# Two blocks on one core: 128 of the 192 tiles of `w_ada` are issued by GpSimd's DMA queue instead of SyncE's

## The chip, the cores and the metric

The kernel runs on one core of one Trainium2 chip. The metric is the device time of one execution in microseconds (us), lower is better. All data is float32 (the engines also use float32r, a form of it that the matrix engine takes in one pass).

## What is computed

The program runs two blocks, one after the other, on 256 tokens of width 2048. The first block is conditioned by a vector `c`: one product `silu(c) @ w_ada + b_ada` gives six rows of 2048 numbers, which shift, scale and gate the two halves of the block. Cut to what matters here:

```
cond = jax.nn.silu(c)
mod = cond @ w_ada[i] + b_ada[i]                      # w_ada: 2048 x 12288
shift1, scale1, gate1, shift2, scale2, gate2 = jnp.split(mod, 6, axis=-1)
h = _modulate(_rms(x, norm1_w[i]), shift1, scale1)
u, q, k, v = jnp.split(h @ w_in[i], splits, axis=-1)
y_ssm = _s5_mixer(u, ...)                             # a scan over the tokens
y_att = _dilated_attention(q, k, v, ...)
x = x + gate1 * (jnp.concatenate([y_ssm, y_att], -1) @ w_out[i])
h2 = _modulate(_rms(x, norm2_w[i]), shift2, scale2)
x = x + gate2 * ((jax.nn.silu(h2 @ w_ffn_gate[i]) * (h2 @ w_ffn_up[i])) @ w_ffn_down[i])
```

The second block has a conditioning product of its own (`ada_w_2`), an attention over the tokens and a context, and a Fourier mixer. All of it works on weights that are read from HBM once.

## The kernel before

**The work on weights.** A weight tile is 512 KB: 256 rows by 512 columns, as 128 partitions by 2 by 512. `gemm` (line 237) walks over the rows; for each tile `wtile` (line 210) loads it into a buffer of the tag `raw` (line 214, issued by SyncE, `SY`), and `split` (line 176) makes two float32r tiles of it: ScalarE casts it into `wh` (line 177), VectorE takes the rest, `wl = raw - wh` (line 178). TensorE then makes twelve products of 128x512 with each tile (line 133). There are three buffers of `wh` and three of `wl`, so at most three split tiles exist at a time. In parts of the first block, weights are used whole, without the split: `full_tile` (line 204) loads them into `wh` or `wl` (line 207).

**The work on the conditioning.** A tile of `w_ada` is also 512 KB and also lives in a `raw` buffer: five buffers (`T["raw"]`) serve both kinds. Tiles are consumed in three ways:

- `ada_tiles` (line 798, issue at line 806) makes the first shift and scale, 64 tiles at the start of the program;
- `ada_gen` (line 296, issue at line 306) takes 128 rows by 1024 columns; VectorE multiplies the tile by one column of `silu(c)` and adds it into an accumulator `acc` (line 278; the first one at line 276). 96 tiles of `w_ada` go this way: both gates, and half of the second shift and scale;
- `ada_quad` (line 347, issue at line 353) takes 256 rows by 512 columns and lets TensorE multiply them, four rows of tokens at a time; 32 tiles of `w_ada`, the other halves of the second shift and scale.

The same `ada_gen` then reads 192 tiles of `ada_w_2` for the second block.

**What sets the order.** `ada_all` (line 383) is a generator, a "lane", that yields after each tile; the loops over weights call `tick()` (line 195) after each weight tile, which advances the lane at a rate set for each stage. In the stage of the hidden layer (`w_ffn_gate`, `w_ffn_up`) the rate is 0.5: one tile of `w_ada` for two weight tiles. The order of the instructions on each engine, and which of the five `raw` buffers a tile gets, are then decided by a scheduler that sorts the program by its own estimates. At run time each engine and each DMA queue takes its instructions strictly in that order, and a DMA into a `raw` buffer waits for the last reader of what lay in it before.

Of the kernel before, what the change touches and what calls it, by code (L numbers as in the profile page):

```python
# [81 lines left out]
def kernel(ctx: ExitStack, tc: tile.TileContext, A, out):  # L82
    nc = tc.nc
    V, S, G, PE, SY = nc.vector, nc.scalar, nc.gpsimd, nc.tensor, nc.sync
# [14 lines left out]
    def uname(s):  # L99
        count[0] += 1  # L100
        return f"{s}_{count[0]}"
# [30 lines left out]
    def mm(o, l, r, start, stop):  # L132
        PE.matmul(o, l, r, start=start, stop=stop)  # L133
# [23 lines left out]
    def rsqrt(src, scale, shape, key="r"):  # L157

        w, y, t, yi = (small(shape, key + n, d) for n, d in (("w", F32), ("y", F32), ("t", F32), ("i", I32)))
        V.tensor_scalar(out=w, in0=src, scalar1=float(scale), scalar2=EPS, op0=ALU.mult, op1=ALU.add)  # L160
        V.tensor_scalar(out=yi, in0=w.bitcast(I32), scalar1=1, scalar2=None, op0=ALU.logical_shift_right)
        V.tensor_scalar(out=yi, in0=yi, scalar1=-1, scalar2=0x5F3759DF, op0=ALU.mult, op1=ALU.add)
        V.tensor_scalar(out=w, in0=w, scalar1=-0.5, scalar2=None, op0=ALU.mult)
        y0 = yi.bitcast(F32)
        for i in range(3):
            if shape[1] == 1:
                V.tensor_scalar(out=t, in0=y0, scalar1=y0, scalar2=w, op0=ALU.mult, op1=ALU.mult)
                V.tensor_scalar(out=y, in0=t, scalar1=1.5, scalar2=y0, op0=ALU.add, op1=ALU.mult)
            else:
                V.tensor_tensor(out=t, in0=y0, in1=y0, op=ALU.mult)  # L170
                V.tensor_tensor(out=t, in0=t, in1=w, op=ALU.mult)
                V.scalar_tensor_tensor(out=y, in0=t, scalar=1.5, in1=y0, op0=ALU.add, op1=ALU.mult)
            y0 = y
        return y
# [98 lines left out]
    def ada_add(acc, raw, vec, kk, first=False):  # L273
        c = condT[:, vec + kk:vec + kk + 1]
        if first:
            V.tensor_scalar(out=acc, in0=raw, scalar1=c, scalar2=None, op0=ALU.mult)
        else:
            V.scalar_tensor_tensor(out=acc, in0=raw, scalar=c, in1=acc, op0=ALU.mult, op1=ALU.add)  # L278
# [7 lines left out]
    def zipped(*gens):  # L286

        gens = list(gens)
        while gens:
            for g in list(gens):  # L290
                try:
                    yield next(g)
                except StopIteration:
                    gens.remove(g)

    def ada_gen(W, bc, col0, vecs, accs, row=False):

        bc = bc + col0 // 128
        if row:
            for j in range(8):  # L300
                S.activation(out=accs[0][:, j * 128:(j + 1) * 128], in_=ident, func=AF.Copy,
                             scale=bcol[:, bc + j:bc + j + 1])
        for kk in range(ND):
            raw = wp.tile([128, 2, 512], F32, name=uname("raw"), tag="raw", bufs=NRAW)
            rf = raw.rearrange("p k n -> p (k n)")
            SY.dma_start(rf, W[kk * 128:(kk + 1) * 128, col0:col0 + 1024])
            for a, v in zip(accs, vecs):
                ada_add(a, rf, v, kk, kk == 0 and not row)
            yield 1.0
# [37 lines left out]
    def ada_quad(b, W, r, c0, n, last):  # L347

        m = 1024 // n
        raws = []  # L350
        for q in range(0, 4, m):
            raw = wp.tile([128, m, n], F32, name=uname("raw"), tag="raw", bufs=NRAW)
            SY.dma_start(raw, W[(r + q) * 128:(r + q + m) * 128, c0:c0 + n].rearrange("(k p) n -> p k n", p=128))
            raws.append(raw)
            yield 1.0
        for j in range(4):
            mm(b[32 * j:32 * j + 32, 0:n], cz[:, r + j], raws[j // m][:, j % m], r == 0, last)

    def ada_pe(W, i, chunks, dst, add, mul=None):

        for c in chunks:
            b = ps_mm()
            for r in range(0, ND, 4):
                yield from ada_quad(b, W, r, i * D + c * 512, 512, r == ND - 4)
            cols = ada_turn(b, 512, 128)
            o = dst[:, c * 4:c * 4 + 4]
            bc = i * ND + c * 4
            V.tensor_reduce(out=o, in_=cols, axis=AX.X, op=ALU.add)
            V.scalar_tensor_tensor(out=o, in0=o, scalar=float(add), in1=bcol[:, bc:bc + 4], op0=ALU.add, op1=ALU.add)
            if mul is not None:  # L370
                V.tensor_tensor(out=o, in0=o, in1=colv[:, mul + c * 4:mul + c * 4 + 4], op=ALU.mult)
# [8 lines left out]
    w_ada = A["w_ada"][0]  # L380
    aw = A["ada_w_2"]

    def ada_all():
        def cols(W, bc, i, v, dst, add):

            accs = [ada_acc() for _ in range(2)]
            yield from zipped(*(ada_gen(W, bc, i * D + h * 1024, [v], [accs[h]]) for h in range(2)))
            ada_cols(accs, [(dst, 8 * h, bc + i * ND + 8 * h) for h in range(2)], add)

        def row(W, bc, i, v, dst):  # L390
            dst += [None] * 2
            accs = [ada_acc() for _ in range(2)]
            yield from zipped(*(ada_gen(W, bc, i * D + h * 1024, [v], [accs[h]], True) for h in range(2)))
            ada_row(accs, dst)

        def half(W, i, dst, add, mul):
            acc = ada_acc()
            yield from ada_gen(W, 0, i * D, [C_C], [acc])
            ada_cols([acc], [(dst, 0, i * ND)], add, mul)
# [496 lines left out]
    r = rsqrt(s1, 1.0 / D, [128, 2])  # L896
# [5 lines left out]
    for c0 in range(0, ND, 2):  # L902
        b = ps_tp()
        for c in range(2):
            for t in range(2):
                o = (c * 2 + t) * 128
                k = c0 + c
# [187 lines left out]
    for nt in range(4):  # L1095
        ps = gemm([(z, 0), (z, 1)], w_out, 0, 8, nt * 512, 512, stagger=3 * (nt == 3))
        for t in range(2):
# [8 lines left out]
            if nt == 3:  # L1106
                s1 = small([128, 1], "s1")
                V.tensor_reduce(out=s1, in_=ssq[t], axis=AX.X, op=ALU.add)
                r = rsqrt(s1, 1.0 / D, [128, 1])
# [689 lines left out]
```

## Time and profile before

| | us |
|---|---|
| runs shown | 2513.39, 2513.71, 2519.57 |
| median of the three | 2513.71 |
| the profiled execution's own time | 2516.57 |
| its span, from the first instruction to the last | 2514.6 |

| engine | busy us | share of the span |
|---|---|---|
| PE (TensorE) | 2379.3 | 95% |
| DVE (VectorE) | 1768.4 | 70% |
| ACT (ScalarE) | 1127.4 | 45% |
| POOL (GpSimd) | 5.6 | 0% |

All DMAs of the program are issued by SyncE (SP in the profile, SPq where its queue is meant); 591 MB are moved, 235 GB/s over the span. A row of the profile names the line of the kernel, the engine, the operation and the tiles (out<-in, without their numbers). "Landing" is when the last part of a DMA's data has arrived, counted from its issue. The stages in order of time, by the issues of their weights: `w_in` to about 375 us, the scan and the first attention with `w_out` to about 560 us, gate and up of the hidden layer from about 565 us to 850 us in its first part, and so on to the Fourier mixer that ends the program.

### The profile page before, as it was taken

How to read it: one execution, taken by the hardware profiler on the slowest of the kernel's cores; microseconds unless marked ns; L12 is line 12 of the kernel's file. 1: busy time of each engine (PE TensorE's matmuls, PEld its weight loads, DVE VectorE, ACT ScalarE, POOL GpSimd, SP SyncE). 2: the span in 40 equal slices, each digit the busy share in tenths (PEclk: the TensorE clock that was granted, in tenths of full speed). 3: DMA queues.
4: the chain of work that ended last, by engine and by line, in shares of the span. 5: the costliest groups of instructions: out<-in, count | busy, mean ns of one | idle time of the engine just before them, and what ended most of it. 6: DMA issues, size and time to landing. Idle time of an engine off the chain costs nothing.

```text
span 2514.6 us, 30153 instructions
## 1 busy us (share of the span) xinstructions
PE 2379.3 (95%) x10791; PEld 1826.3 (73%) x10791; DVE 1768.4 (70%) x2809; ACT 1127.4 (45%) x1770; POOL 5.6 (0%) x7
## 2 busy tenths in 40 slices
PE   5899999989999999999999999999997999999997
PEld 3456645567888778778777878777776778888886
DVE  5876795477668899886777789645678655555557
ACT  3334835355444333434345464555444445444442
POOL 0000000000000000000000000000000000000000
PEclk9888999999999999999999999999998999999999
DMA  9867587877888888888777998634473765665664
GB/s 291 307 241 268 192 300 244 287 253 258 282 272 289 279 290 287 272 257 276 260 250 229 294 302 282 216 102 149 126 261 108 229 212 173 190 198 156 176 209 139
DMA packets 291535, 591.32 MB, mean 235 GB/s; under 512 B 33733, under 2 KB 56617, under 8 KB 291385
## 3 DMA queue, kind: packets, MB, share of 16 engines
q1 hardware_dynamic: 291384, 589.40, 72.1%
q8 instruction: 84, 1.38, 0.2%
q14 instruction: 67, 0.54, 0.1%
HBM read 587.19 MB, written 2.13 MB: 234 GB/s over the span
## 4 chain that ended last, share of the span: by engine, by line
PE 52%; DVE 20%; DMA 18%; issue 5%; ACT 4%; SPq 0%; DVEq 0%; ACTq 0%
PE mm L133 41%; DMA raw<-in_ada_w_dram 14%; PE at L133 7%; DVE wl L178 6%; DVE acc L278 6%; PE tp L133 2%; ACT wh L177 1%; DMA raw<-in_w_ada_dram 1%; DMA raw<-in_w_ffn_down_dram 1%; DMA raw<-in_w_in_attn_dram 1%; PE tp L189 1%; DVE ssm_h L715 1%; DVE wa L278 0%; DVE sl L1570 0%; DVE sl L1573 0%
## 5 line engine op out<-in xcount | busy, mean ns | idle before, releaser
L133 PE MATMUL mm<-wh,s 128*128 128x512 f32 (+3 forms) x4768 | 1464.8, 386 | 2.5 <-ACT wh L177 2.2
L177 ACT CAST wh<-raw 128x1024 fp32r<-128x1024 f32 (+3 forms) x642 | 655.8, 1023 | 900.3 <-PE mm L133 653.4
L133 PEld LDWEIGHTS mm<-wh,s 128*128 128x128 f32 x4768 | 891.4, 189 | 181.8 <-issue 8.6
L178 DVE TENSOR_TENSOR wl<-raw,wh 128x1024 fp32r<-128x1024 f32 (+3 forms) x642 | 756.3, 1186 | 321.0 <-ACT wh L177 319.3
L133 PE MATMUL mm<-wl,s 128*128 128x512 f32 (+3 forms) x2384 | 923.3, 387 | 23.2 <-DVE wl L178 21.4
L278 DVE SCALAR_TENSOR_TENSOR acc<-raw,condT,acc 128x1024 f32<-128x1024 f32 (+2 forms) x413 | 477.7, 1165 | 235.9 <-DMA raw<-in_ada_w_dram 146.4
L133 PEld LDWEIGHTS mm<-wl,s 128*128 128x128 f32 x2384 | 451.3, 189 | 124.6 <-DVE wl L178 38.9
L133 PE MATMUL mm<-wh,sl 128*128 128x512 f32 x536 | 196.2, 459 | 4.5 <-ACT sl L817 2.8
L133 PE MATMUL mm<-wl,sl 128*128 128x512 f32 x440 | 194.9, 521 | 4.3 <-DVE wl L178 2.3
L133 PEld LDWEIGHTS mm<-wh,sl 128*128 128x128 f32 x536 | 100.5, 191 | 56.5 <-issue 32.4
L133 PEld LDWEIGHTS mm<-wl,sl 128*128 128x128 f32 x440 | 82.2, 193 | 68.5 <-issue 51.3
L133 PE MATMUL tp<-wc,sl 128*128 128x128 f32 (+1 forms) x352 | 49.3, 293 | 20.0 <-ACT wc L901 15.3
L133 PEld LDWEIGHTS tp<-wc,sl 128*128 128x128 f32 x352 | 44.9, 199 | 29.8 <-ACT wc L901 15.6
L278 DVE SCALAR_TENSOR_TENSOR wa<-raw,condT,wa 128x512 f32<-128x512 f32 (+1 forms) x75 | 48.2, 642 | 10.1 <-DMA raw<-in_w_ada_dram 9.3
L133 PE MATMUL at<-wl,sl 128*128 128x512 f32 x112 | 52.4, 617 | 0.5 <-DVE sl L864 0.5
L133 PE MATMUL at<-s,s 128*128 128x512 f32 (+1 forms) x96 | 44.8, 647 | 3.9 <-ACT wd L1381 3.3
L133 PEld LDWEIGHTS at<-wl,sl 128*128 128x128 f32 x112 | 21.3, 198 | 26.6 <-issue 21.5
L133 PE MATMUL at<-wh,sl 128*128 128x512 f32 x80 | 36.0, 597 | 0.0
L457 PE MATMUL tp<-ident,sl 128*128 128x128 f32 x64 | 12.0, 337 | 22.7 <-ACT sl L1594 10.5
L189 PEld LDWEIGHTS tp<-ident,wa 128*128 128x128 f32 x208 | 24.5, 141 | 10.4 <-issue 3.3
L189 PE MATMUL tp<-ident,wa 128*128 128x128 f32 x208 | 30.5, 276 | 0.0
L715 DVE TENSOR_TENSOR ssm_h<-ssm_h,ssm_tq 128x64 f32<-128x64 f32 x126 | 27.6, 219 | 1.4
(345 smaller groups left out, 1725.2 us busy)
## 6 DMA issues: line engine op xcount, KB each, us to landing
raw<-in_w_ada_dram SPq DMA_DIRECT2D x192, 512.0 KB, 5.3
raw<-in_ada_w_dram SPq DMA_DIRECT2D x192, 512.0 KB, 4.6
raw<-in_w_in_fourier_dram SPq DMA_DIRECT2D x128, 512.0 KB, 4.1
raw<-in_w_ffn_gate_dram SPq DMA_DIRECT2D x88, 512.0 KB, 4.9
raw<-in_w_ffn_up_dram SPq DMA_DIRECT2D x88, 512.0 KB, 4.7
raw<-in_w_ffn_down_dram SPq DMA_DIRECT2D x88, 512.0 KB, 5.6
raw<-in_w_in_attn_dram SPq DMA_DIRECT2D x72, 512.0 KB, 5.1
raw<-in_w_out_fourier_dram SPq DMA_DIRECT2D x64, 512.0 KB, 4.0
```

Source lines behind the costliest of these rows:

```text
L133: PE.matmul(o, l, r, start=start, stop=stop)
L177: S.copy(hi, src)
L178: V.tensor_sub(lo, src, hi.bitcast(F32))
L189: PE.transpose(b[:, o:o + 128], src(c0 + c, t), ident)
L278: V.scalar_tensor_tensor(out=acc, in0=raw, scalar=c, in1=acc, op0=ALU.mult, op1=ALU.add)
L457: PE.transpose(b[:, c * 128:(c + 1) * 128], xn(4 * g + c, t), ident)
L715: V.tensor_tensor(out=cur, in0=cur, in1=tq[:, :, i], op=ALU.add)
```

## The change

A new function chooses the queue by the tensor that is read, and the two helpers that read conditioning tiles in the lane use it. `ada_tiles`, which makes the first shift and scale, keeps SyncE, and so do all tiles of `ada_w_2`.

```diff
+    def ada_queue(W):
+
+        return G if W is w_ada else SY
+
     def ada_gen(W, bc, col0, vecs, accs, row=False):
...
         for kk in range(ND):
             raw = wp.tile([128, 2, 512], F32, name=uname("raw"), tag="raw", bufs=NRAW)
             rf = raw.rearrange("p k n -> p (k n)")
-            SY.dma_start(rf, W[kk * 128:(kk + 1) * 128, col0:col0 + 1024])
+            ada_queue(W).dma_start(rf, W[kk * 128:(kk + 1) * 128, col0:col0 + 1024])
             for a, v in zip(accs, vecs):
                 ada_add(a, rf, v, kk, kk == 0 and not row)
             yield 1.0
...
     def ada_quad(b, W, r, c0, n, last):
...
             raw = wp.tile([128, m, n], F32, name=uname("raw"), tag="raw", bufs=NRAW)
-            SY.dma_start(raw, W[(r + q) * 128:(r + q + m) * 128, c0:c0 + n].rearrange("(k p) n -> p k n", p=128))
+            ada_queue(W).dma_start(raw, W[(r + q) * 128:(r + q + m) * 128, c0:c0 + n].rearrange("(k p) n -> p k n", p=128))
             raws.append(raw)
             yield 1.0
```

So 96 DMAs of `ada_gen` and 32 of `ada_quad`, 64 MB, leave SyncE's queue for GpSimd's. The lines behind the new function move down by four: 306 becomes 310, 353 becomes 357.

The order on SyncE, in the hidden layer, before: `raw` tiles of `w_ada` stand between the weight tiles, one for two.

```order
L214 DMA raw_940_4279<-in_w_ffn_up_dram 128x2x512
L214 DMA raw_943_4297<-in_w_ffn_up_dram 128x2x512
L306 DMA raw_946_4315<-in_w_ada_dram 128x1024
L214 DMA raw_947_4318<-in_w_ffn_up_dram 128x2x512
L214 DMA raw_954_4342<-in_w_ffn_gate_dram 128x2x512
L306 DMA raw_957_4360<-in_w_ada_dram 128x1024
L214 DMA raw_958_4363<-in_w_ffn_gate_dram 128x2x512
L214 DMA raw_963_4395<-in_w_ffn_gate_dram 128x2x512
L306 DMA raw_966_4413<-in_w_ada_dram 128x1024
```

The order on GpSimd at the same place with the change (before, nothing stands here):

```order
L310 DMA raw_932_4237<-in_w_ada_dram 128x1024
L310 DMA raw_939_4276<-in_w_ada_dram 128x1024
L310 DMA raw_946_4315<-in_w_ada_dram 128x1024
L310 DMA raw_957_4360<-in_w_ada_dram 128x1024
L310 DMA raw_966_4413<-in_w_ada_dram 128x1024
```

SyncE keeps the weight tiles in the same sequence; the tiles of `w_ada` are now in a row of their own on GpSimd.

The order on VectorE in the same stage, one of the few pieces of difference there (line 278 adds a tile of `w_ada`, line 178 makes a `wl`):

```order
 L278 SCALAR_TENSOR_TENSOR acc_3959<-raw_4575,condT,acc_3959 128x1024
 L178 TENSOR_TENSOR wl_4542<-raw_4539,wh_4541 128x1024
+L278 SCALAR_TENSOR_TENSOR acc_3958<-raw_4614,condT,acc_3958 128x1024
 L178 TENSOR_TENSOR wl_4560<-raw_4557,wh_4559 128x1024
-L278 SCALAR_TENSOR_TENSOR acc_3958<-raw_4614,condT,acc_3958 128x1024
 L178 TENSOR_TENSOR wl_4581<-raw_4578,wh_4580 128x1024
 L178 TENSOR_TENSOR wl_4599<-raw_4596,wh_4598 128x1024
```

In three such places of this stage an addition moves ahead of one `wl`; elsewhere in the stage VectorE keeps one addition for two `wl`.

The order on GpSimd around its only other work, three memsets for the scan, with the change:

```order
L310 DMA raw_409_1969<-in_w_ada_dram 128x1024
L310 DMA raw_418_2006<-in_w_ada_dram 128x1024
L777 MEMSET ssm_h_281_1380 32x32x32
L777 MEMSET ssm_h_281_1380 32x32x64
L777 MEMSET ssm_h_281_1380 32x32x96
L310 DMA raw_419_2009<-in_w_ada_dram 128x1024
L310 DMA raw_429_2048<-in_w_ada_dram 128x1024
```

Before, the memsets (then line 773) were alone on GpSimd; now the fifteenth tile of `w_ada` and all later ones stand behind them.

## Rows read from the trace of the kernel before

**Rows 1.** The page: the span, and busy time by engine.

```profile
span 2514.6 us, 30153 instructions
PE 2379.3 (95%) x10791; PEld 1826.3 (73%) x10791; DVE 1768.4 (70%) x2809; ACT 1127.4 (45%) x1770; POOL 5.6 (0%) x7
```

**Rows 2.** Instructions on `in_w_ada_dram`, whole span: count, duration ns, first and last start.

```profile
L306 SPq DMA_DIRECT2D raw<-in_w_ada_dram x96: 327/341/607, 201.4 to 731.2; - x96
L353 SPq DMA_DIRECT2D raw<-in_w_ada_dram x32: 367/378/460, 328.7 to 546.9; - x32
```

**Rows 3.** Stretches: PE, PEld, DVE, ACT, POOL busy (x), granted clock, DMA share, GB/s.

```profile
188.00:251.00 63.00, 60.48 (x238) 41.38 (x236) 43.00 (x74) 25.28 (x51) 5.41 (x3) 0.88 0.76 265
251.00:314.00 63.00, 62.46 (x253) 39.54 (x253) 48.89 (x190) 51.86 (x126) 0.00 (x0) 0.90 0.57 194
...
629.00:692.00 63.00, 63.00 (x284) 52.28 (x283) 42.60 (x38) 27.31 (x29) 0.00 (x0) 1.00 0.86 282
```

**Rows 4.** The chain that ended last, 574 to 760 us: start, us, what.

```profile
621.38 43.55 PE mm L133 x192
664.93 0.87 PE tp L189 x8
```

**Rows 5.** VectorE's timeline, 641 to 649 us: start, us, instruction, idle before and releaser.

```profile
641.44 1.28 DVE L278 SCALAR_TENSOR_TENSOR acc<-raw,condT,acc 128x1024 f32<-128x1024 f32 x1 [0.89 <-DMA raw<-in_w_ada_dram]
...
644.28 1.23 DVE L178 TENSOR_TENSOR wl<-raw,wh 128x1024 fp32r<-128x1024 f32 x1 [0.42 <-ACT wh L177]
646.48 1.28 DVE L278 SCALAR_TENSOR_TENSOR acc<-raw,condT,acc 128x1024 f32<-128x1024 f32 x1 [0.97 <-DMA raw<-in_w_ada_dram]
647.68 1.22 DVE L178 TENSOR_TENSOR wl<-raw,wh 128x1024 fp32r<-128x1024 f32 x1
```

**Rows 6.** Instructions on `in_w_ada_dram`, 592 to 732 us: count, who waited, landing.

```profile
L306 SPq DMA_DIRECT2D raw<-in_w_ada_dram x26: 340/340/341, 592.6 to 731.2; - x26
...
  DVE acc L278: 27.8, 26
...
DMA to landing us min/median/max: 3.5/4.2/4.9
```

**Rows 7.** Waits of SyncE's queue, 592 to 732 us: total us, times, longest.

```profile
SPq L306 <- DVE acc L278: 33.0, 26, 1.4
```

**Rows 8.** ScalarE's timeline, 643 to 647 us.

```profile
643.19 1.05 ACT L177 CAST wh<-raw 128x1024 fp32r<-128x1024 f32 x1 [1.67 <-PE mm L133]
645.91 1.05 ACT L177 CAST wh<-raw 128x1024 fp32r<-128x1024 f32 x1 [1.67 <-PE mm L133]
```

**Rows 9.** The chain that ended last, 1125 to 1245 us: shares, then first and last pieces.

```profile
by line: DMA raw<-in_ada_w_dram 75.4%; DVE acc L278 20.6%; issue 2.2%; DVE wl L178 2.0%; DVE acc L276 0.6%; DVEq L278 0.0%; DVE col L329 0.0%
...
1136.39 3.80 DMA raw<-in_ada_w_dram
...
1238.85 4.45 DMA raw<-in_ada_w_dram
```

**Rows 10.** GpSimd's memsets, line 773: duration ns, first and last start.

```profile
L773 POOL MEMSET ssm_h<- x3: 946/1802/2661, 238.6 to 241.4; 32x1024 f32 x1, 32x2048 f32 x1, 32x3072 f32 x1
```

**Rows 11.** SyncE's timeline, 244 to 246 us.

```profile
244.52 1.37 SPq L306 DMA_DIRECT2D raw<-in_w_ada_dram  x3
```

**Rows 12.** All waits of VectorE, 300 to 400 us: total us, times, longest.

```profile
DVE sl L753 <- ACT sl L753: 10.0, 8, 3.8
...
```

**Rows 13.** The chain that ended last, 540 to 575 us.

```profile
558.55 0.07 DVE col L371
```

**Rows 14.** Waits of TensorE, 200 to 574 us (eleven rows): the longest, and the only DMA.

```profile
PE tp L457 <- DVE wa L462: 5.2, 2, 3.4
...
PE mm L133 <- DMA wl<-in_w_in_dram: 0.6, 1, 0.6
```

## The prediction

> **What bounds the kernel now.** I read the page first, for the engine that sets the time: PE is busy for 2379.3 of 2514.6 us, VectorE for 1768.4 [rows 1]. TensorE therefore sets the time, unless something makes it wait. Next I asked where the moved DMAs lie: 96 on line 306 and 32 on line 353, issued between 201 and 732 us [rows 2]. Then I read stretches and chain there. The hidden layer is the strictest place: from 629 to 692 us PE is busy for 63.00 of 63.00 us at a granted clock of 1.00 [rows 3], and the chain is PE alone, 43.55 us for 192 products and 0.87 us of transposes [rows 4]. At twelve products to a weight tile that is 16 tiles in 44.42 us, or **5.55 us for two weight tiles**.
>
> Third, VectorE's timeline there. Its pattern is one addition of a `w_ada` tile (1.28 us), then two `wl` (1.22 us each); the addition starts when its DMA lands, after 0.89 or 0.97 us idle [rows 5]. Last, who holds that DMA back. SyncE's queue waited for the previous addition 26 times, 33.0 us in all [rows 7]: there are 26 such DMAs in the stretch, each goes out only when the addition before it has ended, and VectorE waits for every one of them [rows 6]. The other four `raw` buffers are in use for weights, so the conditioning tiles run through one buffer: issue, landing after a median of 4.2 us, addition, next issue. From 592.6 to 731.2 us there are 25 rounds [rows 6], so **a round takes 5.54 us**, and it brings one tile of `w_ada` for two weight tiles. The round and TensorE, at 5.55 us, are neck and neck.
>
> **The change part by part.**
>
> *Issues taken from SyncE.* 96 x 0.34 + 32 x 0.37 = 45 us [rows 2]. I count this at nothing: in the hidden layer SyncE mostly stands waiting for buffers [rows 7], and what covers it is TensorE's work. If the cover is gone, in the waits before 574 us, see the second rival. GpSimd's own busy time before is 5.6 us [rows 1], so it has room for 128 issues.
>
> *GpSimd's queue order.* Its three memsets now stand ahead of the fifteenth tile. They end at 241.4 + 2.66 = 244.1 us [rows 10], and SyncE issued the DMAs that now stand behind them at 244.5 us [rows 11]: no cost. Past this point only `w_ada` tiles stand on GpSimd, so a tile that waits for a buffer holds up only other tiles of `w_ada`; weights no longer stand behind it on SyncE. In the hidden layer that frees weights that are early anyway.
>
> *VectorE's order.* Three times in the hidden layer an addition moves ahead of one `wl`. That makes one `wl` later by at most the addition and its wait, 1.28 + 0.97 = 2.25 us [rows 5], inside the spare worked out below: nothing by itself.
>
> *Time from release to landing.* This is the term that counts. Call λ what GpSimd's way adds to it. No DMA from GpSimd is in the trace, so I bound λ. From below: a queue of its own could let each tile land in the shortest time seen, 3.5 in place of 4.2 us [rows 6], λ = -0.7; the round would then be 4.8 us, TensorE would still need 5.55, and the gain is nothing. From above: the nearest rows of GpSimd doing anything are its memsets, 0.95, 1.80 and 2.66 us [rows 10]; SyncE's issue, which falls away, is 0.34 [rows 6]. If GpSimd takes as long to make the 128 rows of a transfer as for one of them, λ is 0.6, 1.5 or 2.3. I take **λ = 1.0**, about midway between 0.6 and 1.5, since a transfer of 128 rows writes far less than the longer memsets do.
>
> What λ costs: the next DMA is released by the addition, which waits for the previous one, so λ enters every round. VectorE works in order, so the two `wl` behind an addition come later with it. ScalarE's casts, which TensorE releases, start at 643.19 and 645.91 us [rows 8]; the `wl` that belong to them end at 644.28 + 1.23 = 645.51 and 647.68 + 1.22 = 648.90 [rows 5], 2.32 and 2.99 us after the release, while TensorE has the two other split tiles, 5.55 us, to work on. The spare is 3.2 and 2.6 us; I take 2.6, once. Each round then takes 5.54 + 1.0 = 6.54 against 5.55:
>
> 26 x (6.54 - 5.55) = 25.7; less the spare, 2.6; and λ once more, 1.0, where the last tiles of the second scale end on the chain [rows 13], before the hidden layer can begin. **Sum: +24.1 us.**
>
> At λ = 2.3 it is 26 x 2.29 - 2.6 + 2.3 = +59; at λ = 0.38, 26 x 0.37 - 2.6 + 0.4 = +7.4. That a round can set the time here is seen later in the program: from 1125 to 1245 us the same loop with `ada_w_2` is the chain, 75.4% DMA and 20.6% addition, and from the DMA at 1136.39 to that at 1238.85 there are 18 rounds of 5.69 us [rows 9]. That is 0.15 us more than 5.54, enough for the loop to take over.
>
> Between 300 and 400 us the moved tiles cost nothing: VectorE waits there for no DMA at all, but for ScalarE, 10.0 us [rows 12].
>
> The Trainium skill (DMA: Bandwidth & Descriptors, section "Anatomy of one DMA — SWDGE (gpsimd) path") fits a GpSimd DMA as 2.0 us plus bytes/436e3, an estimate of 3.2 us for 512 KB. The rows show 4.2 us from SyncE beside other traffic [rows 6]; by the fit λ would be negative and the sum zero. The case below, that GpSimd is as fast, has its chance partly for that.
>
> The execution of the profile took 2516.6 us, 2.9 more than the median of the runs shown. 2516.6 + 24.1 - 2.9 = **2538 us** (2537.8).
>
> **The rivals.**
>
> *No change:* λ is below 0.38. For it: the buffer wait is satisfied in the same way, the bytes are the same, and PE at 63.00 of 63.00 [rows 3] forgives anything that stays below the tie and the spare. Against it: a tie at 5.54 to 5.55 forgives only what λ takes from 2.6 us, and that is 0.1 us per round. Time: 2513.7, give or take 7.5 us, which is 0.3% and about what a measurement of this kernel can tell from no change. Chance 0.20. The Trainium skill (DMA: Bandwidth & Descriptors, section "Specifications") gives a first byte after some 1 us from GpSimd against 0.6 from SyncE; the estimate with λ = 0.4 is 26 x 0.39 - 2.6 + 0.4 = +7.9 us, between this rival and the forecast.
>
> *Faster:* SyncE's line is shorter from 201 to 574 us, weights no longer stand behind `w_ada` tiles that wait, and TensorE's waits there shrink. They sum to 17.9 us in eleven rows; but the longest, 5.2 us, is for VectorE, and only 0.6 us is for a DMA [rows 14]. From 188 to 314 us the clock was 0.88 and 0.90 [rows 3]; with steady work, (1 - 0.88) x 60.48 + (1 - 0.90) x 62.46 = 13.5 us would come back. Half of the waits is 9 us: 2505. It decides if λ is below 0.1 and 7.5 us or more come back. Chance 0.08. The Trainium skill (DMA: Bandwidth & Descriptors, section "Issuing engines are not separate DMA queues") says that issuing from several engines saves only the sequencer's time; by that this rival gets nothing, as [rows 14] already suggest.
>
> *Much slower:* VectorE's instructions hold up GpSimd while it makes the descriptors. In the hidden layer SyncE's DMA goes out when the addition ends, and at once a `wl` of 1.22 us starts [rows 5]. If GpSimd must wait for it and then needs 1.0 us, λ is about 2.3: +59, 2573 us. For it: VectorE is busy for 42.60 of 63 us there [rows 3]. Against it: nothing in this trace shows such a lock. Chance 0.10. The Trainium skill (SBUF — State Buffer, section "Who interferes with whom") has such starvation for copies and casts, but infers that an operation with two tensors takes only the read side, which making descriptors does not need. By that, this case falls away; no run here shows it yet.
>
> **How the numbers follow.** The forecast, λ between 0.38 and about 2, has 0.62: 2521 to 2565 us; no change 0.20, much slower 0.10, faster 0.08. Since the no-change case and the forecast's low end meet, the range runs from 2511, just below the median, to 2573, the upper bound of λ; it leaves out most of the faster case, a little of the no-change case and the worst of the slow one. Faster by over 0.3%: 0.08. Within 0.3%: 0.20. Slower: 0.62 + 0.10 = 0.72.
>
> **What would show it.** Right: in the hidden layer, from 592 us on, the tiles of `w_ada` on GpSimd land 5 us or more after the end of the addition that releases them; their starts lie about 6.5 us apart; the chain from 600 to 735 us goes over DMA and additions in place of PE alone; VectorE's wait for these tiles grows from 27.8 us [rows 6] to about 50; and PE is busy for less than 63.00 in 63 us. The loss lies before 750 us, and the time from there to the end is as before. Wrong: the rounds keep 5.55 us and PE stays whole, so that λ is within the spare; or the loss is at 240 to 560 us, where GpSimd's waiting would hold up tiles that SyncE had brought in time; or the schedule gives these tiles a second buffer, so that the issue runs ahead of the addition and λ is hidden.

## The result, and the profile after

| | before | with the change |
|---|---|---|
| median of the runs | 2513.55 us | 2549.88 us |
| runs | 2512.2 to 2519.57 | 2547.38 to 2550.93 |
| ratio of the times | | 1.0138, interval 1.012 to 1.0156 |
| the profiled execution, its span | 2514.6 us [rows 1] | 2548.2 us |

The change costs 36 us. The page of the changed kernel, span and engines, shows TensorE busy for 18 us more [rows 1], although its work is the same, for part of the time at a lower granted clock (see the last section); GpSimd's 81 us are almost all DMA issues.

```profile
span 2548.2 us, 30237 instructions
PE 2397.6 (94%) x10791; PEld 1839.0 (72%) x10791; DVE 1765.8 (69%) x2809; ACT 1126.7 (44%) x1770; POOL 81.1 (3%) x135
```

The instructions on `w_ada` over the whole span (count, shortest, median and longest in ns, first and last start) answer to [rows 2]: an issue takes 0.53 or 0.72 us on GpSimd, where it took 0.34 or 0.37 on SyncE.

```profile
L310 POOL DMA_DIRECT2D raw<-in_w_ada_dram x96: 528/531/1001, 198.5 to 765.9; - x96
L357 POOL DMA_DIRECT2D raw<-in_w_ada_dram x32: 717/719/719, 327.7 to 571.5; - x32
```

In the hidden layer the same view over 617 to 768 us holds the 26 tiles that answer to [rows 6]; the second piece is the waits of VectorE from 300 to 400 us (total, times, longest), which answer to [rows 12], where no DMA was waited for.

```profile
L310 POOL DMA_DIRECT2D raw<-in_w_ada_dram x26: 528/531/531, 617.3 to 765.9; - x26
...
  DVE acc L278: 56.4, 26
...
DMA to landing us min/median/max: 3.7/4.0/6.9
```

```profile
DVE sl L757 <- ACT sl L757: 12.6, 5, 7.0
DVE acc L278 <- DMA raw<-in_w_ada_dram: 10.7, 6, 4.6
```

Two things stand out. The landing's median is 4.0 us, shorter than SyncE's 4.2, and GpSimd starts a DMA 0.29 us after the end of the addition that releases it (663.05 to 663.35 us, for one) where SyncE took 0.03 (642.72 to 642.75). So the tiles are not late as a rule; a round takes (765.9 - 617.3) / 25 = 5.94 us on average, but only because a few are long. And there are waits before 400 us that were not there.

Where the time goes is best read from how far TensorE is behind. Both kernels give it the same 10791 instructions, between the 900th and the 1600th in places in another order, from the 2000th on in the same one; the table takes the start of the k-th of them and subtracts the start in the first profile of before. The other rows are the experiments below, each from its one profiled execution.

| k-th instruction of TensorE | 900 | 1100 | 1300 | 1600 | 2000 | 2300 | 2800 | 3600 | 10791 |
|---|---|---|---|---|---|---|---|---|---|
| its start before, us | 293 | 356 | 395 | 478 | 579 | 646 | 756 | 941 | 2501 |
| the change | 3.9 | 9.5 | 15.8 | 22.0 | 23.3 | 26.6 | 35.3 | 33.9 | 33.2 |
| e1, queue only | 4.7 | 4.6 | 15.4 | 15.7 | 16.0 | 16.0 | 16.0 | 16.1 | 5.6 |
| e2, order only | 5.7 | 6.1 | 15.2 | 17.7 | 14.8 | 17.3 | 19.3 | 19.1 | 17.3 |
| e3, hidden layer only | 2.7 | 2.9 | 12.0 | 12.3 | 12.1 | 17.3 | 23.4 | 23.9 | 18.5 |
| e4, before it only | 2.1 | 9.6 | 18.6 | 25.6 | 26.9 | 26.9 | 27.0 | 27.3 | 15.4 |
| e5, three pairs put back, first seam | 5.1 | 13.0 | 14.0 | 26.0 | 37.8 | 41.7 | 41.7 | 43.4 | 31.0 |
| e6, queue only, hidden layer only | -0.2 | -0.3 | 10.5 | 10.6 | 10.6 | 11.2 | 12.4 | 12.4 | 3.1 |
| e7, before once more | 0.5 | 1.3 | 8.7 | 9.0 | 10.4 | 10.4 | 10.5 | 11.6 | 3.7 |
| e8, e1 once more | 0.2 | 0.2 | 12.3 | 12.3 | 15.1 | 16.9 | 16.9 | 17.0 | 4.7 |
| e9, three pairs put back, second seam | -0.9 | 6.5 | 11.5 | 17.9 | 20.9 | 21.0 | 21.0 | 20.4 | 16.8 |
| e10, late on purpose, 1024 | 0.1 | 0.0 | 10.8 | 10.8 | 11.0 | 30.1 | 70.2 | 71.0 | 64.4 |
| e11, late on purpose, 512 | 3.1 | 3.0 | 3.4 | 3.5 | 1.7 | 15.3 | 39.3 | 39.3 | 28.1 |

The change falls behind in four steps: 5.6 us between the 900th and the 1100th instruction, 6.3 from there to the 1300th, 6.2 from there to the 1600th, and 12.0 us in the hidden layer, from the 2000th to the 2800th. The step from the 1100th to the 1300th is no effect of the change alone: the kernel before falls back by 7.4 us there itself in its second profile (e7; see the last section). The last column holds a trap, too. Behind 941 us the first profile of before loses some 8 us that e7 keeps (11.6 to 3.7); from 1698.3 to 1761.2 us, for one, its granted clock is 0.92 and that of e7 1.00. So a lag at the 3600th instruction is not yet a difference of total times.

### The profile page after: what moved, and what is told of

Same layout as the page of the kernel before. It is cut to its first block, busy times and chain, and to the rows that moved or that the text cites. A ratio compares the mean times of both kernels' runs of the same rounds, so it can differ in the third digit from the quotient of the medians.

```text
span 2548.2 us, 30237 instructions
## 1 busy us (share of the span) xinstructions
PE 2397.6 (94%) x10791; PEld 1839.0 (72%) x10791; DVE 1765.8 (69%) x2809; ACT 1126.7 (44%) x1770; POOL 81.1 (3%) x135
## 4 chain that ended last, share of the span: by engine, by line
PE 33%; DMA 17%; DVE 14%; issue 5%; ACT 2%; DVEq 0%; SPq 0%; ACTq 0%; POOLq 0%
PE mm L133 28%; DMA raw<-in_ada_w_dram 14%; DVE wl L178 5%; DVE acc L278 4%; PE at L133 2%; DMA raw<-in_w_in_attn_dram 1%; PE tp L133 1%; ACT wh L177 1%; DMA raw<-in_w_ffn_down_dram 1%; PE tp L189 0%; DVE sl L1574 0%; DVE sl L1577 0%; PE tp L1399 0%; DVE wb L1227 0%; ACT sl L485 0%
## 5 line engine op out<-in xcount | busy, mean ns | idle before, releaser
L133 PE MATMUL mm<-wh,sl 128*128 128x512 f32 x536 | 201.8, 470 | 7.4 <-ACT sl L177 4.2
L310 POOL DMA_DIRECT2D raw<-in_w_ada_dram x96 | 52.6, 548 | 586.1 <-ACT ssm_w L628 198.0
L133 PE MATMUL tp<-wc,sl 128*128 128x128 f32 (+1 forms) x352 | 50.3, 297 | 19.8 <-ACT wc L905 15.3
L189 PEld LDWEIGHTS tp<-ident,wa 128*128 128x128 f32 x208 | 24.5, 141 | 11.8 <-issue 3.3
L461 PE MATMUL tp<-ident,sl 128*128 128x128 f32 x64 | 12.5, 350 | 21.7 <-ACT sl L1598 10.5
L757 ACT COPY sl<-at 32x128 f32<-32x128 f32 x32 | 12.2, 382 | 45.9 <-PE at L133 39.2
```

The source lines that it names most:

```text
L189: PE.transpose(b[:, o:o + 128], src(c0 + c, t), ident)
L310: ada_queue(W).dma_start(rf, W[kk * 128:(kk + 1) * 128, col0:col0 + 1024])
L461: PE.transpose(b[:, c * 128:(c + 1) * 128], xn(4 * g + c, t), ident)
L757: copy(uT[half][32 * q:32 * q + 32, 2 * h8:2 * h8 + 2, i:256:4], b[32 * i:32 * i + 32].rearrange("p (k q n) -> p q k n", k=2, q=4)[:, q])
```

## The experiments

Three theories were put against each other. The **latency theory** is the prediction's: GpSimd's way adds λ to every round of the hidden layer. The **order theory**: the scheduler, once another engine issues the tiles, puts work on VectorE and TensorE in another sequence and gives tiles other buffers, and that costs the time. The **collision theory**: two queues let transfers start together, and the tile that is needed first lands late.

To separate queue and order, some kernels hold the order: a table lists each engine's instructions in the order that another kernel had, and order-only dependencies (no wait at run time) chain them; the raw buffer of each tile is held by five tags in place of one.

```diff
         tile_two_blocks_kernel(tc, args, o)
+        _in_order(tc, nc)
...
+                tc.add_manual_dep(i, last.name, mybir.DependencyInfo(mybir.DependencyClass.NoSync, mybir.DependencyReason.DATA), reason='order')
...
-        raw = wp.tile([128, 2, 512], F32, name=uname("raw"), tag="raw", bufs=NRAW)
+        raw = wp.tile([128, 2, 512], F32, name=uname("raw"), tag=raw_slot(), bufs=1)
```

These helpers move line numbers: in the kernels that hold the order the addition is line 283, and the issue in `ada_gen` line 315 (311 in e2, 317 in e10 and e11).

**e1, the queue alone.** Order and buffers of before; the 128 DMAs from GpSimd. The latency theory is used here with the numbers read in the trace of the change, by which nothing is added; the prediction's own λ of 1.0 is tested by the rounds.

> The kernel before with the order of every engine and the raw buffer of every tile held as they were, by tables; only the 128 DMAs go out from GpSimd. Latency theory (each round of the hidden layer longer by what GpSimd adds): after that trace, GpSimd starts 0.28 us after the release and lands a median of 4.0 us later, SyncE 0.03 and 4.2, so nothing is added and the time is 2513 +- 8. Order theory (the scheduler places the work otherwise once another engine issues the tiles, and that costs the time): 2513 +- 8. Collision theory (two queues let weights and w_ada tiles start together, and the tile that is needed first lands late): 2535 to 2550, with 20 us or more lost between 300 and 500 us.

Measured: 2526.39 us, ratio 1.0058 (1.0035 to 1.0082), +15.5 us on 2510.86. That is above the 2521 at which both the order theory and the latency theory ended and below the collision theory's 2535, so the total bears out none of the three. In the hidden layer TensorE loses nothing (16.0, 16.0, 16.0 in the table). The 26 tiles of e1 there:

```profile
L315 POOL DMA_DIRECT2D raw<-in_w_ada_dram x26: 528/528/531, 610.0 to 749.3; - x26
...
  DVE acc L283: 39.8, 26
...
DMA to landing us min/median/max: 3.7/3.9/4.8
```

A round is (749.3 - 610.0) / 25 = 5.57 us against 5.54 before [rows 6]: GpSimd's queue adds 0.03 us, not 1.0. The prediction's λ falls. VectorE's wait for these tiles is 39.8 us, 12 more than before, and costs nothing: a long wait for a tile is no loss by itself. The 15.5 us between the medians are not located. The profiled execution of e1 lies 16 us behind at the end of the hidden layer, 10.8 of them from the 1100th to the 1300th instruction, where e7 falls back too; at the end of the program it is 5.6 us behind, and e7 3.7.

**e2, the order alone.** Order and buffers of the change, all DMAs on SyncE; only the place of a `w_ada` tile among SyncE's other DMAs is the scheduler's choice.

> The kernel before, all DMAs on SyncE, with the order of PE, VectorE, ScalarE and of SyncE's other DMAs and the raw buffers held as the change has them; where a w_ada tile stands between the others on SyncE is left to the scheduler. Order theory: 2540 to 2555, most of the +36 us. Collision theory: 2513 +- 10, since one queue serves the transfers in turn again. Latency theory: 2513 +- 10.

Measured: 2535.82 us, 1.0087 (1.006 to 1.0114), +25 us. It is over the ±10 us of the two other theories and short of the order theory's 2540. In the hidden layer it loses 4.5 us where the change loses 12.0, and between the 900th and the 1100th instruction 0.4 us where the change loses 5.6. So the order costs something on SyncE as well, but its full price needs GpSimd's queue beside it. Of e2's other lag, 9.1 us are the step from the 1100th to the 1300th instruction, which e7 has too, and 5.7 us lie before the 900th and were not taken apart.

**e3 and e4, the two halves of the change.**

```diff
-    def ada_queue(W):
-        return G if W is w_ada else SY
+    def ada_queue(W, c):
+        return G if W is w_ada and c >= 5 * D else SY
...
```

> Only the 32 tiles of the second gate (columns from 10240 on, issued from 560 us) go to GpSimd; all before them stays on SyncE. Latency theory as predicted, +1 us a round: about 2538. Order theory: TensorE's order is as before, 24 lines of VectorE's differ; +6 to +11 us (2520 to 2525), in steps of 2 to 4 us at the places where an addition stands ahead of one wl and after three. Collision theory: +0 to +11.

> Only the 96 tiles of first gate, second shift and second scale go to GpSimd; the second gate stays on SyncE. Latency theory as predicted: +1 us or nothing (2514). Order theory and collision theory both: the part of the loss before 560 us, +20 to +25 (2534 to 2539).

(e4 has `c < 5 * D`.) Measured: e3 2527.77 us, 1.0053 (1.0028 to 1.0077); e4 2536.67 us, 1.0096 (1.0066 to 1.0126). e4 is where the order and the collision theory wanted it; e3's total lies above the order theory's 2525 and below the latency theory's 2538, with runs from 2517 to 2538. The halves add up: 17 + 26 = 43 against the change's 36, within their intervals. In e3 TensorE loses 11.3 us in the hidden layer, just past the order theory's upper end of 11.

**e6, the queue alone in the hidden layer.** As e1, but only the 32 tiles of the second gate leave SyncE.

> The kernel before with order and raw buffers held, only the 32 tiles of the second gate go out from GpSimd. Up to 560 us it is the kernel before. Order theory: as before, 2511 +- 5, in rounds of 5.55 us. Latency theory: +26 x what GpSimd adds; at 1 us, 2537.

Measured: 2521.63 us, 1.0026 (1.0004 to 1.0048). The time is above the expected 2511 ± 5, but not in the hidden layer: TensorE loses 1.8 us there, and 10.8 us between the 1100th and the 1300th instruction, where the program is still that of before. Against e3 the only difference is the held order and buffers, and 11.3 us become 1.8.

**e5 and e9, the change with three pairs put back.** In the hidden layer the orders of VectorE differ in three places and nowhere else: an addition stands ahead of one `wl` in place of behind it. Both kernels keep the change's order and buffers up to a seam and take those of before behind it.

> The change with its own order and raw buffers held by tables up to the hidden layer; in the hidden layer the order and the buffers of the kernel before: on VectorE three additions stand again behind the wl beside them, nothing else moves there. All 128 tiles stay on GpSimd. Order theory: the 11 us that the change loses between 600 and 770 us are gone, so 2539 +- 5, and the rounds take 5.55 us. Latency theory: no difference from the change, 2550.

Measured: 2549.05 us, 1.0146 (1.0102 to 1.019): a miss by the total. TensorE's lag stays at 41.7 us from the 2300th to the 2800th instruction, as the order theory wants, but between the 1970th and the 1985th it had jumped by 10.5 us: TensorE waited 11.8 us, in one piece, for line 471 at the seam of the two orders. So the seam was moved.

> As the fifth experiment, with the seam between the two orders moved into the hidden layer, between its first and its second third, ahead of the first of the three pairs: up to there order and buffers are the change's, behind it the kernel before's; all 128 tiles from GpSimd. Order theory: TensorE's lag behind the kernel before stays what it is at 640 us to the end of the hidden layer (the change adds 11 us there), time 2539 +- 5 against the change's 2550. Latency theory: the lag grows by 1 us a round as the prediction had it, or by what the change adds, 2550.

Measured: 2534.58 us, 1.0089 (1.0063 to 1.0115): 15 us less than the change, at the low end of what was expected. The stretches of e9 in the hidden layer, and then the change's (columns as in [rows 3]):

```profile
640.00:700.00 60.00, 60.00 (x274) 49.85 (x273) 43.22 (x40) 25.16 (x27) 5.84 (x11) 1.00 0.85 287
700.00:760.00 60.00, 60.00 (x271) 49.76 (x270) 41.12 (x38) 26.31 (x28) 5.31 (x10) 1.00 0.86 288
```

```profile
640.00:700.00 60.00, 57.67 (x261) 47.06 (x260) 41.67 (x40) 24.49 (x27) 5.56 (x11) 1.00 0.80 271
700.00:760.00 60.00, 56.71 (x252) 46.16 (x251) 38.40 (x35) 24.18 (x26) 5.57 (x11) 1.00 0.79 264
```

TensorE is whole again, with every tile still on GpSimd. **The hidden layer's 12 us are the three pairs** and the buffers that go with them; the two were put back together, so their shares are read from the rows of the change below.

**e7 and e8, before and e1 once more.**

> The kernel before, unchanged, for a second look at the small products at the end of the scan (369 to 383 us in its first profile, at the full clock). If the half clock there is a matter of chance in every one of these kernels, this look has it or not, and the other stretches agree with the first profile within 2 us; time 2505 to 2524.

> The kernel of the first experiment (order and buffers of before, 128 DMAs from GpSimd), for a second look. If GpSimd's queue itself costs time in a fixed place, TensorE falls behind before's at the same place as in the first look; if the 15 us are the clock, the half clock at the end of the scan shows again and nothing else of over 2 us after 200 us.

Measured: 2520.27 and 2521.78 us, one execution each. The kernel before now has the half clock, too, and falls back by 7.4 us between the 1100th and the 1300th instruction (1.3 to 8.7); that the other stretches agree within 2 us held up to 941 us and not behind it. e8 falls back by 12.1 us there and by 2.8 and 1.8 us before and in the hidden layer; the +4.7 us that e1 had before 293 us are not in e8, so they were no fixed cost. At the end of the program e1, e8 and e7 are 5.6, 4.7 and 3.7 us behind the first profile of before: in the profiled executions the queue alone costs 2 us or less against e7. Whether it makes the half clock likelier (e1's median is 15.5 us above that of before) is open.

**e10 and e11, late on purpose.** If λ is not there, is the prediction's price for it right? In e6, GpSimd first sets part of the buffer to zero; the DMA behind it overwrites that. (`_EXTRA` only keeps the new instruction out of the tables that hold the order.)

```diff
+            if W is w_ada and col0 >= 5 * D:
+                _EXTRA.append(G.memset(rf[:, 0:1024], 0.0).ins.name)
             ada_queue(W, col0).dma_start(rf, W[kk * 128:(kk + 1) * 128, col0:col0 + 1024])
```

> The sixth experiment (only the 32 tiles of the second gate from GpSimd, order and buffers of before) with a time from release to landing made longer on purpose: GpSimd first sets all 1024 columns of the raw buffer to zero, which the DMA then overwrites. By the memsets in the first trace that takes about 0.95 us and the hand-over, so each round is 6.5 to 6.7 us long. If the prediction's formula holds: 26 x (6.6 - 5.55) - 2.6 = +25 us on the sixth experiment, between 2540 and 2550, and the chain there goes over DMA, memset and addition. If the queue has spare that the formula lacks: less than half of it.

> As the tenth, with 512 columns: about 0.5 us and the hand-over, rounds of 6.0 to 6.2 us. By the formula 26 x (6.1 - 5.55) - 2.6 = +12 us on the sixth experiment, 2530 to 2538, half of what the tenth adds. If rounds have spare: +0 to +5.

Measured: e10 2575.25 us, 1.0252 (1.0207 to 1.0296); e11 2558.78 us, 1.0181 (1.0153 to 1.0208). Both miss, upwards: e10 loses 59 us in the hidden layer (11.0 to 70.2), e11 38 (1.7 to 39.3). The chain of e10 there, one round of it (start, us, what):

```profile
661.72 0.96 POOL raw L316
662.68 0.29 issue
662.97 5.00 DMA raw<-in_w_ada_dram
667.97 0.02 issue
667.99 1.30 DVE acc L283
669.29 0.05 issue
```

And the tiles of e10 in the hidden layer, then those of e11:

```profile
L317 POOL DMA_DIRECT2D raw<-in_w_ada_dram x26: 530/530/532, 599.8 to 795.0; - x26
...
DMA to landing us min/median/max: 4.6/5.0/6.5
```

```profile
L317 POOL DMA_DIRECT2D raw<-in_w_ada_dram x25: 527/527/530, 605.7 to 772.2; - x25
...
DMA to landing us min/median/max: 4.2/4.4/6.2
```

Rounds are (795.0 - 599.8) / 25 = 7.81 and (772.2 - 605.7) / 24 = 6.94 us. Put into the prediction's formula: 26 x (7.81 - 5.55) - 2.6 = 56 and 26 x (6.94 - 5.55) - 2.6 = 34 us, against 59 and 38 measured. **The price of a round is right; what makes a round long was not.** The memset and its hand-over add 0.96 + 0.05 = 1.01 us (the 0.29 us ahead of the DMA are there in e1 as well), but the round grows by 7.81 - 5.57 = 2.24: the landing itself gets longer, in the mean of the 26 tiles from 3.95 (e1) to 5.18 us, in the median from 3.9 to 5.0. The timeline of SyncE in e10 shows what is different there:

```profile
647.06 0.37 SPq L219 DMA_DIRECT2D raw<-in_w_ffn_gate_dram  x1
```

A weight tile goes out at 647.06 us, 0.15 us ahead of e10's DMA of `w_ada` at 647.21, and so it is in 25 of the 26 rounds. In before (642.75, then 643.88 and 645.53 us) and in e1 (665.17, then 666.04 and 667.17) the tile of `w_ada` is ahead of the two weight tiles of its round, in e1 by 0.87 us in each of the 26 rounds; in e11 it is ahead by 0.28 us, with a median of 4.4 us to land. So the order of start and the landing go together (0.87 us ahead: 3.9, 0.28 ahead: 4.4, 0.15 behind: 5.0); that it is the cause was not tested by itself. The Trainium skill (DMA: Bandwidth & Descriptors, section "Issuing engines are not separate DMA queues") says that transfers of all issuing engines interleave on the same DMA engines; e10 agrees, with 1.1 us more to land for the tile that starts second.

## Why the prediction was right or wrong

The time, 2549.9 us, lies in the range of 2511 to 2573, and in the forecast's own 2521 to 2565; slower was given 0.72. That the number came out is luck: the 25.7 us of the term that counted are not there, and costs that were put at nothing took their place.

- **What bounds the kernel** held. The round and TensorE are neck and neck: e10 and e11 show that all that is added to a round lands on the end, at about the price that was worked out.
- **"Time from release to landing", λ = 1.0: this step failed.** Measured, it is 5.57 - 5.54 = 0.03 us a round (e1), below the 0.6 that was the low end of the three values from memsets, and above the stated lower bound of -0.7. GpSimd takes 0.53 us for the issue, the first packet on its queue starts 1.24 us after the issue began (median of the change's 26 tiles), and the last part lands after 3.9 us (e1): none of it is a wait of a memset's length on top of SyncE's 4.2. The memset rows [rows 10] were a poor neighbour: they show GpSimd filling memory, not making a transfer. The 25.7 us of the sum are not in the trace. The Trainium skill's fit (DMA: Bandwidth & Descriptors, section "Anatomy of one DMA — SWDGE (gpsimd) path") gave 3.2 us for 512 KB; the measured 3.9 to 4.0 is more, but its verdict on λ, that the sum of this term is zero, was the better one.
- **"VectorE's order: nothing by itself": this step failed**, and it is where the hidden layer's 12.0 us come from: 3.1, 4.1 and 3.9 us at the three places, 0.9 before them. VectorE of the changed kernel at the first of them (as [rows 5]), TensorE, and GpSimd's DMAs there:

```profile
661.76 1.29 DVE L278 SCALAR_TENSOR_TENSOR acc<-raw,condT,acc 128x1024 f32<-128x1024 f32 x1 [1.97 <-DMA raw<-in_w_ada_dram]
662.97 1.22 DVE L178 TENSOR_TENSOR wl<-raw,wh 128x1024 fp32r<-128x1024 f32 x1
667.26 1.28 DVE L278 SCALAR_TENSOR_TENSOR acc<-raw,condT,acc 128x1024 f32<-128x1024 f32 x1 [3.08 <-DMA raw<-in_w_ada_dram]
668.47 3.49 DVE L178 TENSOR_TENSOR wl<-raw,wh 128x1024 fp32r<-128x1024 f32 x3
675.97 1.28 DVE L278 SCALAR_TENSOR_TENSOR acc<-raw,condT,acc 128x1024 f32<-128x1024 f32 x1 [4.01 <-DMA raw<-in_w_ada_dram]
```

```profile
669.74 0.50 PE L133 MATMUL mm<-wl,s 128*128 128x512 f32 x1 [2.08 <-DVE wl L178]
```

```profile
663.35 0.53 POOL L310 DMA_DIRECT2D raw<-in_w_ada_dram  x1 [5.00 <-DVE acc L278]
669.98 0.53 POOL L310 DMA_DIRECT2D raw<-in_w_ada_dram  x1 [6.10 <-DVE wl L178]
```

  One `wl` stands between two additions in place of two, then three follow. The larger part is direct. The prediction counted 1.28 + 0.97 = 2.25 us, with the wait that an addition had in the old order. In the new place the `wl` that used to fill the time until the tile lands stands behind the addition, whose wait is 3.08 us: the `wl` comes 1.28 + 3.08 = 4.36 us later, against a spare of 2.6. TensorE stands still for 2.08 us until that `wl` ends at 669.68, and for 2.08 and 1.97 us at the two other places (717.22 and 765.62 us). With these waits its lag grows by 2.4, 2.4 and 2.3 us, 7.1 in all.

  The smaller part comes one tile later. The buffer that the addition at 667.26 frees now takes a weight tile (SyncE sends it at 668.58); the next tile of `w_ada` gets a buffer that the first of the three `wl` frees, so its DMA goes out at 669.98 instead of about 668.8, behind that weight tile, and lands after 6.0 us (675.94), not 3.8. From addition to addition it is 8.71 us, where the two weight tiles of a round last 5.55. The lag grows by another 0.7, 1.7 and 1.6 us behind the three places. On SyncE the same order costs 4.5 us (e2).
- **"Between 300 and 400 us the moved tiles cost nothing": failed.** The row of before was read as if its order would stay. In the change VectorE's additions stand earlier among most of the scan's steps, and the tiles land later (7.8 us in the median of the ten from 330 to 360 us, 6.5 before). One addition waits 4.63 us, and the scan and ScalarE's row scaling behind it wait with it. VectorE, ScalarE and TensorE of the changed kernel:

```profile
355.10 1.28 DVE L278 SCALAR_TENSOR_TENSOR acc<-raw,condT,acc 128x1024 f32<-128x1024 f32 x1 [4.63 <-DMA raw<-in_w_ada_dram]
```

```profile
357.80 1.28 ACT L1005 ACTIVATE sl<-sl,rhy 128x128 f32<-128x128 f32 x4 [7.77 <-DVE rhy L172]
```

```profile
358.25 1.20 PE L189 MATMUL tp<-ident,sl 128*128 128x128 f32 x6 [2.62 <-ACT sl L1005]
```

  It takes both: with GpSimd's queue and the order of before (e1) VectorE waits 1.4 us for these DMAs from 300 to 400 us, with that order on SyncE (e2) 7.2, with both 10.7, and TensorE loses -0.1, 0.4 and 5.6 us. The cost is thus shown to need both; why the scheduler puts the additions earlier was not tried.
- **A cost that no term of the prediction has** lies from the 1300th to the 1600th instruction: 6.2 us in the change, 7.0 and 6.4 in e4 and e9, which share its order there and GpSimd's queue, 2.5 in e2, and 0.3 or less in the kernels with the order of before (e1, e6, e7, e8). Half of it is one wait of TensorE at 500 us:

```profile
PE mm L133 <- ACT sl L177: 4.2, 1, 4.2
```

  In the change two casts of weight tiles stand on ScalarE ahead of the two casts of `sl` that TensorE needs, and they wait for their DMAs (494.71 and 497.20 us); in before the casts of `sl` stand first. The prediction compared orders in the hidden layer and on GpSimd only.
- **λ once more at the second scale, +1.0:** not there; the lag does not grow between the 1600th and the 2000th instruction by more than before's own second profile, e7, does (1.3 and 1.4 us).
- **The rival "no change"** had its condition met (λ of 0.03 is below 0.38) and yet was wrong, because it took the order as given.
- **The rival "faster"** came to nothing: the clock from 188 to 314 us is 0.87 and 0.86, not above [rows 3], and both queues still wait for buffers.
- **The rival "much slower"** came to nothing: in the hidden layer a `wl` starts beside each issue, and all 26 issues take 528 to 531 ns. The Trainium skill (SBUF — State Buffer, section "Who interferes with whom") infers that an operation with two tensors does not starve GpSimd's descriptors; these rows agree.
- **What would show it:** the first sign, tiles on GpSimd landing 5 us or more after the release, was wrong (0.29 + 4.0 = 4.3 as a rule), and the starts lie 5.94 us apart in the mean, not 6.5. That PE is busy for less than the whole (57.67 of 60.00 us) came true, by the three places and not by λ. VectorE's wait for the tiles grew to 56 us, close to the 50 that were named as a sign of λ; e1, with 40 us and no loss, shows that it was no sign. The loss did end before 770 us, but two thirds of it lie before 560 us, named under "wrong".

The sum, then: the change's lag of 35.3 us at the end of the hidden layer is 12.0 us from the three pairs on VectorE, 5.6 from the additions among the scan and 6.2 from the order between the 1300th and the 1600th instruction, 23.8 us in all that go with the order; 6.3 us where before loses 7.4 in part of its executions; 3.9 us before 293 us, where e1 and e8, the same kernel twice, differ by 4.5; and 1.3 us between the 1600th and the 2000th. The executions of before bear this out from another side. Over the 41 beside the experiments, time and mean granted clock go together: a straight line through them gives 2.0 us for each 0.001 of the clock, with a scatter of 2.6 us. At the change's 0.969 the line, led on by 0.001, gives 2525 us for before, so about 25 of the 36 us are not the clock. This is an estimate; whether the lower clock is itself a consequence of the change was not tested.

## What to carry to other kernels

Where a scheduler decides, the engine that issues a DMA is no local choice: compare the order of all engines and the buffers, and price each moved instruction with the wait that it will meet in its new place (3.08 us here, not the 0.97 of the old one), and with what it does to the next transfer that it releases. To separate a queue from the order that comes with it, hold the order by order-only dependencies and the buffers by tags; here that turned 12.0 us into 0.1 (e9). In a one-buffer loop that is level with the engine it feeds, count who goes out first after the release: with the tile 0.15 us behind a weight tile it took 1.1 us longer to land.

## What was unexpected of the hardware

**The clock falls, or not, in the same program.** At the end of the scan TensorE has about 10 us of products of 63 and 64 columns, after a wait of 1.5 to 1.8 us. The stretches 379 to 384 and 384 to 389 us (columns as in [rows 3]) of the first profile of before, and of its second, e7:

```profile
379.00:384.00 5.00, 5.00 (x41) 4.05 (x43) 2.30 (x5) 1.45 (x4) 0.00 (x0) 1.00 0.34 108
384.00:389.00 5.00, 4.38 (x26) 1.75 (x18) 3.64 (x8) 3.57 (x9) 0.00 (x0) 1.00 0.61 205
```

```profile
379.00:384.00 5.00, 5.00 (x26) 5.00 (x25) 2.04 (x3) 1.03 (x3) 0.00 (x0) 0.50 0.21 80
384.00:389.00 5.00, 5.00 (x25) 5.00 (x25) 0.38 (x1) 0.11 (x1) 0.00 (x0) 0.50 0.36 108
```

At a granted clock of 1.00 (2.4 GHz) these products last from 372.32 to 382.66 us; in e7, where the clock falls to 0.50 (1.2 GHz) at about 376 us, they last from 373.57 to 390.77: 10.3 and 17.2 us, with the same instructions in the same order. Of 41 executions of before beside the experiments, 30 have a mean clock of 0.974 or more and a median of 2510.6 us, 11 a lower one and 2520.6 us; the changed kernel's four are at 0.969 and 0.970. All profiles but the first of before and e11 show the half clock here. Whether the change makes it likelier, as the counts suggest, or which stretches the 11 lost their time in, was not settled. By the straight line of the sum above e1, whose median is 15.5 us above that of before, is 7 us above it at equal clock.

**GpSimd's DMAs are as quick as SyncE's** in this loop: 0.29 us from release to start and 3.9 us to land (e1), against 0.03 and 4.2, although the issue itself is 0.19 us longer.
